# A hybrid attention and RG-LRU block: the T blocks of X made by four operations and begun sooner, the first chunks of X loaded once, three of seven low parts made by GpSimd in the second half

## The chip, the core and the metric

One core of one Trainium2 chip. The metric is device time in microseconds. Engines are named as in the profile: PE (TensorE matmuls), PEld (its weight loads), DVE (VectorE), ACT (ScalarE), POOL (GpSimd), SP (SyncE, which here only issues DMAs).

## The reference

The core of what is computed, for x of (1, 2048, 1024):

```python
proj = x @ w_in[l] + b_in[l]                    # 1024 -> 9216 columns: q, k, v, two SiLU gates, LRU input, merge gates
q, k, v, g_attn, u_lru, g_lru, gate_logits = jnp.split(proj, SPLIT_POINTS, axis=-1)
...                                             # rotary q and k, dilated banded attention for 3 groups of 8 heads
y_a = attn @ w_attn_proj[l]
u = causal_depthwise_conv(u_lru, conv_w[l], conv_b[l])
h = rg_lru(u, ...)                              # gates, then a scan over positions
y_b = (h * jax.nn.silu(g_lru)) @ w_lru_proj[l]
gates = jax.nn.sigmoid(gate_logits).reshape(B, S, N_BRANCHES, D)
merged = gates[:, :, 0] * y_a + gates[:, :, 1] * y_b
x = layer_norm(DEEPNORM_ALPHA * x + merged @ w_out[l] + b_out[l], ln_gain[l], ln_bias[l])
```

The change lies in the first line, the projection; everything behind it stays as it is.

## The kernel before, in words

The kernel runs in stages: the projection (to about 1555 us), attention, the two output projections with the gates, and the last product with the layer norm. Only the projection matters here.

**Products.** The 9216 columns are 72 strips of 128. Two strips make a pair, and the positions are taken in two halves of 1024, each of two chunks of 512; so the plan has 72 pairs, 0 to 35 for the first half and 36 to 71 for the second. Of a pair, weights (two strips by two halves of the inner dimension: A11, A12, A21, A22) and X (two halves of the inner dimension by two chunks: B11, B12, B21, B22) are 2 by 2 blocks. The first pair of each half is done plainly in eight products. All others take seven, by the scheme of Strassen and Winograd: `UNIT` and `BLK` give for product numbers 1 to 7 the weight block (A11, A12, S4, A22, S1, S2, S3) and the X block (B11, B21, B22, T4, T1, T2, T3). S1 to S4 and T1 to T4 are sums of blocks. The order of a pair's products is a tuple: `MID = (1, 6, 7, 5, 2, 4, 3)`, and `EDGE` for a half's last pair. In this document the first, second, ... seventh product of a pair is counted in that order.

**High and low parts.** For accuracy each block is split into a rounded high part (ACT copies it) and a low part (DVE or POOL subtracts). A product is twelve matmuls in `product` (L605): for each of four K tiles of 128, high by high, high by low, and the low part of the weights by high. So the low part of a weight block, tile `l`, is wanted by the third matmul of its product. Four `l` buffers hold two low parts each.

**The clock of the program.** One product is one tick. Per tick the code issues the product, then the events planned for it, then what chains (rotary products, gates, LRU) have come due, then the evacuation of PSUM. Each engine runs its own queue in this order, without a scheduler; events are put at ticks by hand (`at`). For a pair whose first product is at tick b, weights are loaded on SP ten to six ticks before (`load_w`); S1 and S3 are made by DMAs that accumulate into a loaded block, issued by POOL (`added`); `sums` makes S2 (DVE) and S4 (DVE in the first half, POOL in the second); `prep_w` makes high and low part of one unit per tick, four ticks ahead of its product in the first half, three in the second.

**Low parts of the second half.** In the first half `prep_w` makes the low parts (POOL the even ones, DVE the odd ones) and stores them to DRAM, `wl_scr`: two of 512 x 128 fp32 each (512 KB) after units 1, 3 and 5 and one (256 KB) after unit 6, counted from 0. In the second half `load_lo` (L290) reads them back, issued on SP for units 0, 2, 4 and 6; no low part of these pairs is computed.

**T blocks.** `comb` takes one K tile of the four raw blocks (tiles `xcB`) and makes T1, T2, T3 and the raw T4 with five sums on DVE, three copies on ACT, two low parts on POOL (T1, T3) and one on DVE (T2). `fourth` splits T4 later. At the start, the raw chunks for this are loaded a second time (`comb_loads`, 16 loads of 256 KB), four K tiles over ticks 0 to 3, and the four `comb` stand at ticks 3 to 6. At the change of halves, E0 is seven ticks before pair 36; loads stand at E0 + 6 to 9 and `comb` at E0 + 9 to 12.

Of the kernel before, what the change touches and what calls it, by code (L numbers as in the profile page):

```python
# [15 lines left out]
P = 128  # L16
# [4 lines left out]
CH = 512  # L21
# [10 lines left out]
def hybrid_block_kernel(ctx: ExitStack, tc: tile.TileContext, a: dict, out: bass.AP):  # L32
# [3 lines left out]
    def flat(t):  # L36
        return t.bitcast(F32)
# [13 lines left out]
    qk_scr = {(n, u): dram.tile([P, S], F32, name=f"{n}_scr{u}") for u in range(12) for n in ("qh", "ql", "k")}  # L51


    wl_scr = [dram.tile([P, 7, CH], F32, name=f"wl_scr{p}") for p in range(36)]
    u_scr = [dram.tile([P, CH], F32, name=f"u_scr{i}") for i in range(8)]


# [50 lines left out]
    def later(lag, fn):  # L108
        late.append((now["n"] + lag, fn))
# [23 lines left out]
    XSLOT = {"B11": "X2", "B21": "X3", "T2": "X4", "T3": "X5", "T1": "X1", "T4": "X0", "B12": "X0", "B22": "XA"}  # L133

    PLAIN = [(fi, k, c) for c in range(2) for fi in range(2) for k in range(2)]
    MID, EDGE = (1, 6, 7, 5, 2, 4, 3), (1, 2, 6, 7, 4, 5, 3)

    stA = ctx.enter_context(ExitStack())
    sl_p = stA.enter_context(tc.tile_pool(name="sl_p", bufs=1))
# [14 lines left out]
    def give(*ts):  # L154
        for t in ts:
            vacant.append(home.pop(id(t))[0])
# [69 lines left out]
        sp.dma_start(r, a["xT"][:, kx, c * CH:(c + 1) * CH])  # L226

    def drop_raw(b, kk):
        give(xr.pop((b, kk)))

    def tt(eng, out, in0, in1, op):
        eng.tensor_tensor(out=out, in0=in0, in1=in1, op=op)  # L232
# [30 lines left out]
    def prep_w(s, j):  # L263

        n = units_of(s)[j]
        r = raw.pop((s, n))
        h = take(f"h{n}_{s}")
        act.activation(h, r, AF.Copy)  # L268
        spend(ACT=.66)
        if (s, j // 2) not in LO:  # L270
            LO[s, j // 2] = take_lo(f"l{j}_{s}")
        l = LO[s, j // 2][1][:, j % 2]
        if plan[s][2] is None or not plan[s][0]:
            eng = pool if j % 2 == 0 else dve
            tt(eng, l, r, flat(h), ALU.subtract)
            if eng is pool:
                spend(POOL=1.55)
            else:
                spend(DVE=.93)
        give(r)  # L280
        U[s, n] = (h, l)
        if plan[s][2] and not plan[s][0] and (j % 2 or j == 6):
            jj = j - j % 2
            t = LO[s, j // 2][1][:, 0:j - jj + 1]
            later(2, lambda: sp.dma_start(wl_scr[plan[s][3]][:, jj:j + 1], flat(t)))

    def load_lo(s, j):
        t = LO[s, j // 2] = take_lo(f"l{j}_{s}")
        n = 1 if j == 6 else 2
        sp.dma_start(flat(t[1][:, 0:n]), wl_scr[plan[s][3]][:, j:j + n])  # L290
# [247 lines left out]
    plan = []  # L538
    for h in range(2):
        for p, (kind, f0, f1) in enumerate(seq):  # L540
            plan.append((h, ((f0, kind), (f1, kind)), None if p == 0 else EDGE if p == len(seq) - 1 else MID, p, kind))
# [113 lines left out]
    def at(t, fn):  # L655
        events.setdefault(t, []).append(fn)

    for s in range(1, NQ):
        t0 = base[s] - (3 if plan[s][0] else 4)
        if plan[s][2] is None:  # L660
            for d, n in ((4, "A21"), (4, "A11"), (3, "A22"), (3, "A12")):
                at(t0 - d, lambda s=s, n=n: load_w(s, n))
            for j in range(4):
                at(t0 + j, lambda s=s, j=j: prep_w(s, j))
            continue
        for d, n in ((6, "S1"), (6, "S3"), (4, "A11"), (3, "A22"), (3, "A12")):
            at(t0 - d, lambda s=s, n=n: load_w(s, n))
        at(t0 - 4, lambda s=s: added(s, "S1", "A22"))
        at(t0 - 4, lambda s=s: added(s, "S3", "A11"))
        at(t0 - 1, lambda s=s: sums(s))  # L670
        for j in range(7):
            if plan[s][0] and j % 2 == 0:
                at(t0 + j - 1, lambda s=s, j=j: load_lo(s, j))
            at(t0 + j, lambda s=s, j=j: prep_w(s, j))
    for s, pl in enumerate(plan):
# [23 lines left out]
    def comb(kk):  # L699
        r11, r12, r21, r22 = (xr["c" + b, kk] for b in ("B11", "B12", "B21", "B22"))  # L700
        if kk == 0:
            for n in ("T1", "T2", "T3"):
                new_block(n)
        tt(dve, r11, r11, r12, ALU.subtract)
        tt(dve, r12, r22, r12, ALU.subtract)
        hi_lo("T1", kk, r11, pool)
        tt(dve, r21, r11, r21, ALU.subtract)
        hi_lo("T3", kk, r12, pool)
        tt(dve, r11, r11, r22, ALU.add)
        hi_lo("T2", kk, r11, dve)  # L710
        tt(dve, r21, r21, r22, ALU.add)
        for b in ("B11", "B12", "B22"):
            drop_raw("c" + b, kk)
        spend(ACT=2.0, DVE=4.3, POOL=2.8)

    def fourth(kk):
        if kk == 0:
# [122 lines left out]
    for b in ("B12", "B22"):  # L840
        for kk in K4:
            load_raw(b, 1, kk)
    early = events
    events = {}
    prep_w(0, 0)
# [1 line left out]
        one_block("B11", 0, kk, some(kk))  # L847
    at(0, lambda: prep_w(0, 1))
    at(0, lambda: [one_block("B21", 0, kk, some(kk)) for kk in K4])
    at(0, lambda: comb_loads(0, 0))  # L850
    at(1, lambda: prep_w(0, 2))
    at(1, lambda: comb_loads(0, 1))
    at(1, lambda: prep_w(0, 3))
    at(2, lambda: [one_block("B12", 1, kk, some(kk)) for kk in K4])
    at(2, lambda: comb_loads(0, 2))
    at(3, lambda: [one_block("B22", 1, kk, some(kk)) for kk in K4])
    at(3, lambda: comb_loads(0, 3))
    for kk in K4:
        at(3 + kk, lambda kk=kk: comb(kk))
    at(7, lambda: [fourth(kk) for kk in K4])  # L860
# [519 lines left out]
```

## Time and profile before

| | us |
|---|---|
| median of 3 runs | 2367.07 |
| lowest, highest | 2362.84, 2371.19 |
| the profiled execution | 2367.64 |
| its span | 2365.8 |
| PE busy | 2243.7 (95%) |
| DVE, ACT, POOL busy | 1726.1 (73%), 1084.9 (46%), 1014.7 (43%) |
| DMA moved | 551.48 MB, 233 GB/s |

The profile is of one execution. A timeline row gives start and duration in us, engine, line, operation, what it writes and reads, and in brackets how long the engine stood idle before it and what ended that. A row of waits gives the total, the number and the longest. Matmul durations overlap: three of 0.39 us each start within 0.68 us.

### The profile page before, as it was taken

The numbers are of one execution on the slowest core, as the hardware profiler recorded it, in microseconds if no ns is written. First come the engines' busy times: TensorE is split into PE (matmuls) and PEld (weight loads), VectorE is DVE, ScalarE is ACT, GpSimd is POOL, SyncE is SP. The second block draws the span as 40 slices with busy tenths as digits, with TensorE's granted clock in tenths as the row PEclk, the third lists the DMA queues.
The fourth block names the chain that finished last, engine by engine and source line by source line (L and its number), as shares of the span: only waits on it lengthen the run. The fifth ranks groups of instructions, "written<-read, shape, count | busy, mean of one in ns | idle before, by whom it ended". The sixth has DMA issues, their size and how long they took to land.

```text
span 2365.8 us, 34610 instructions
## 1 busy us (share of the span) xinstructions
PE 2243.7 (95%) x11008; PEld 1878.5 (79%) x11008; DVE 1726.1 (73%) x3116; ACT 1084.9 (46%) x1977; POOL 1014.7 (43%) x760
## 2 busy tenths in 40 slices
PE   6999999999999799999999999989999999979998
PEld 4788888888788687787787877779999878758886
DVE  7888888899888676676667777546666558857677
ACT  4346445455465455465456665446666611121100
POOL 5554554456545433223232232368666326532220
PEclk8999999999999899999999999989999999999999
DMA  6888997988988987898897888897886579874431
GB/s 237 238 260 236 271 286 230 265 258 265 269 260 295 287 245 229 240 245 233 230 252 244 268 241 255 253 255 191 214 211 162 162 233 304 269 241 155 157 116 63
DMA packets 347174, 551.48 MB, mean 233 GB/s; under 512 B 99056, under 2 KB 140016, under 8 KB 342384
## 3 DMA queue, kind: packets, MB, share of 16 engines
q1 hardware_dynamic: 308160, 489.80, 66.2%
q0 software_dynamic: 20160, 36.71, 9.5%
q10 hardware_dynamic: 18672, 22.75, 3.1%
q8 instruction: 88, 1.44, 0.3%
q14 instruction: 94, 0.77, 0.1%
HBM read 343.81 MB, written 180.16 MB: 221 GB/s over the span
## 4 chain that ended last, share of the span: by engine, by line
PE 61%; DMA 13%; DVE 10%; issue 7%; POOL 4%; ACT 3%; SPq 2%; ACTq 0%; DVEq 0%; POOLq 0%
PE q L605 43%; DMA l<-wl_scr 4%; PE o L978 3%; PE s L939 2%; DMA A<-qh_scr 2%; PE pt L954 1%; PE yb L1167 1%; PE yb L1168 1%; PE yb L1166 1%; PE z L1260 1%; PE z L1258 1%; PE z L1259 1%; DVE xcB L232 1%; POOL C L789 1%; DMA wA<-in_w_in_dram 1%
## 5 line engine op out<-in xcount | busy, mean ns | idle before, releaser
L605 PE MATMUL q<-xT,hS 128*128 128x512 f32 x1680 | 523.3, 393 | 10.5 <-ACT hS L268 6.1
L605 PE MATMUL q<-xT,l 128*128 128x512 f32 x1120 | 438.9, 392 | 3.2 <-DVE l L232 3.2
L605 PE MATMUL q<-xB,hA 128*128 128x512 f32 x1248 | 398.7, 401 | 19.1 <-ACT hA L268 11.5
L605 PE MATMUL q<-xB,l 128*128 128x512 f32 x904 | 362.2, 401 | 36.8 <-DMA l<-wl_scr 28.2
L605 PEld LDWEIGHTS q<-xT,hS 128*128 128x128 f32 x1680 | 317.0, 189 | 78.7 <-ACT hS L268 7.1
L605 PEld LDWEIGHTS q<-xB,hA 128*128 128x128 f32 x1248 | 240.5, 194 | 70.6 <-ACT hA L268 12.3
L605 PEld LDWEIGHTS q<-xT,l 128*128 128x128 f32 x1120 | 211.7, 189 | 48.9 <-DVE l L232 4.3
L605 PEld LDWEIGHTS q<-xB,l 128*128 128x128 f32 x904 | 173.9, 192 | 81.4 <-DMA l<-wl_scr 35.1
L945 ACT ACTIVATE p<-p,osb 128x256 f32<-128x256 f32 (+1 forms) x384 | 156.5, 455 | 114.1 <-DVE osb L943 113.4
L232 POOL TENSOR_TENSOR sw<-sw,sin 128x512 f32<-128x512 f32 x96 | 159.8, 1681 | 98.6 <-DMA sw<-y 96.5
L943 DVE CUSTOM_DVE_ANT_0 p<-s,mask 128x256 f32<-128x256 f32 (+1 forms) x384 | 125.1, 364 | 100.4 <-PE s L939 59.6
L250 POOL DMA_DIRECT2D wS<-in_w_in_dram x140 | 123.8, 994 | 169.8 <-DMA wS<-in_w_in_dram 103.0
L268 ACT ACTIVATE hA<-wA 128x512 fp32r<-128x512 f32 x218 | 134.9, 623 | 95.3 <-DMA wA<-in_w_in_dram 51.1
L605 PE MATMUL q<-xB,hS 128*128 128x512 f32 x560 | 175.4, 394 | 2.1 <-DVE v L232 2.0
L605 PE MATMUL q<-xT,hA 128*128 128x512 f32 x560 | 174.1, 392 | 0.2 <-DVE u L232 0.2
L978 PE MATMUL o<-V,ptb 128*128 128x65 f32 x1200 | 165.0, 276 | 9.7 <-ACT ptb L959 7.8
L232 POOL TENSOR_TENSOR S<-S,wA 128x512 f32<-128x512 f32 x35 | 50.1, 1433 | 281.6 <-DVE S L232 116.3
L978 PEld LDWEIGHTS o<-V,ptb 128*128 128x128 f32 x1200 | 151.7, 194 | 21.4 <-ACT ptb L959 19.4
L232 DVE TENSOR_TENSOR y<-y,cos 128x512 f32<-128x512 f32 x96 | 121.3, 1267 | 48.6 <-DMA sw<-y 48.3
L232 POOL TENSOR_TENSOR l<-wA,hA 128x512 fp32r<-128x512 f32 x74 | 116.6, 1576 | 55.7 <-ACT hA L268 37.7
L1232 POOL TENSOR_TENSOR me<-gA,ybr 128x512 f32<-128x512 f32 x32 | 47.8, 1507 | 180.1 <-DVE gA L1231 177.6
L605 PEld LDWEIGHTS q<-xB,hS 128*128 128x128 f32 x560 | 104.3, 189 | 24.8 <-issue 2.9
(190 smaller groups left out, 4995.2 us busy)
## 6 DMA issues: line engine op xcount, KB each, us to landing
wA<-in_w_in_dram SPq DMA_DIRECT2D x218, 256.0 KB, 5.6
wl_scr<-l SPq DMA_DIRECT2D x105, 512.0 KB, 4.9
l<-wl_scr SPq DMA_DIRECT2D x105, 512.0 KB, 6.2
wS<-in_w_in_dram SPq DMA_DIRECT2D x140, 256.0 KB, 4.9
wS<-in_w_in_dram POOLq DMA_DIRECT2D x140, 256.0 KB, 7.0
sw<-y SPq DMA_DIRECT2D x384, 64.0 KB, 3.7
mg_scr<-y SPq DMA_DIRECT2D x59, 256.0 KB, 5.9
o_scr<-osb ACTq DMA_DIRECT2D x48, 264.0 KB, 5.9
```

Of the source, the lines that this page charges most:

```text
L232: eng.tensor_tensor(out=out, in0=in0, in1=in1, op=op)
L250: pool.dma_start(t, w_part(s, x), accum_op=ALU.add)
L268: act.activation(h, r, AF.Copy)
L605: pe.matmul(bank, w[:, ks], x[:, kk, xx], start=(first and i == 0), stop=(last and i == 11))
L789: pool.tensor_tensor(out=b2[hs, h, t], in0=flat(b2[hs, h, t]), in1=flat(B1[hs, h, t]), op=ALU.subtract)
L939: pe.matmul(s[:, h, (0 if g == 2 and n else lo):256], q, k, start=(i == 0), stop=(i == 1))
L943: dve.tensor_tensor_reduce(out=p[:, h, lo:256], in0=s[:, h, lo:256], in1=mask[:, lo:256], scale=1.0, scalar=3e38, op0=ALU.add, op1=ALU.min ...
L945: act.activation(p[:, h, lo:256], p[:, h, lo:256], AF.Exp, scale=-1.0, bias=mm)
L954: pe.transpose(pt[:, 2 * h + x, :], p[:, h, x * P:(x + 1) * P], ident)
L978: pe.matmul(o[:, n % 2, h * 65:h * 65 + 65], ptb[:, 2 * h + x, :], V[:, kb, vo + h * 65:vo + h * 65 + 65], start=(x == lo // P), stop=(x = ...
L1166: pe.matmul(yb, WL[f][:, 0, k], xx[:, 0], start=(k == 0), stop=False)
L1232: pool.tensor_tensor(out=ME[c][:, f], in0=ga, in1=yb, op=ALU.add)
```

## The change

- The pair after a plain one (pairs 1 and 37) takes the order `FIRST = (1, 2, 6, 7, 5, 4, 3)`: B21 before T2.
- `comb` makes the T blocks with four sums: T2 goes into B22's raw tile, and the raw T4 is T2 - B21. T1's low part goes to DVE and POOL in turn.
- At the start the raw chunks are kept and `comb` reads them; the second loads go. The blocks B12 and B22 are split one tick sooner, and `added` for pair 1 stands at tick 2 instead of 0. `comb` stays at ticks 3 to 6.
- At the change of halves loads for `comb` and `comb` stand two ticks sooner.
- In the second half units 0, 1 and 6 get their low part from POOL; only units 2 to 5 are stored and read back.

```diff
-    wl_scr = [dram.tile([P, 7, CH], F32, name=f"wl_scr{p}") for p in range(36)]
+    wl_scr = [dram.tile([P, 4, CH], F32, name=f"wl_scr{p}") for p in range(36)]
-    MID, EDGE = (1, 6, 7, 5, 2, 4, 3), (1, 2, 6, 7, 4, 5, 3)
+    MID, EDGE, FIRST = (1, 6, 7, 5, 2, 4, 3), (1, 2, 6, 7, 4, 5, 3), (1, 2, 6, 7, 5, 4, 3)
...
     def drop_raw(b, kk):
-        give(xr.pop((b, kk)))
+        t = xr.pop((b, kk))
+        if xr.get(("c" + b, kk)) is not t:
+            give(t)
...
         l = LO[s, j // 2][1][:, j % 2]
-        if plan[s][2] is None or not plan[s][0]:
-            eng = pool if j % 2 == 0 else dve
+        if plan[s][2] is None or not plan[s][0] or j in (0, 1, 6):
+            eng = pool if j % 2 == 0 or plan[s][0] and plan[s][2] else dve
             tt(eng, l, r, flat(h), ALU.subtract)
...
-        if plan[s][2] and not plan[s][0] and (j % 2 or j == 6):
-            jj = j - j % 2
-            t = LO[s, j // 2][1][:, 0:j - jj + 1]
-            later(2, lambda: sp.dma_start(wl_scr[plan[s][3]][:, jj:j + 1], flat(t)))
+        if plan[s][2] and not plan[s][0] and j in (3, 5):
+            t = LO[s, j // 2][1]
+            later(2, lambda: sp.dma_start(wl_scr[plan[s][3]][:, j - 3:j - 1], flat(t)))
...
-        n = 1 if j == 6 else 2
-        sp.dma_start(flat(t[1][:, 0:n]), wl_scr[plan[s][3]][:, j:j + n])
+        sp.dma_start(flat(t[1]), wl_scr[plan[s][3]][:, j - 2:j])
...
-        at(t0 - 4, lambda s=s: added(s, "S1", "A22"))
-        at(t0 - 4, lambda s=s: added(s, "S3", "A11"))
+        for n, x in (("S1", "A22"), ("S3", "A11")):
+            at(max(t0 - 4, 2), lambda s=s, n=n, x=x: added(s, n, x))
...
-            if plan[s][0] and j % 2 == 0:
+            if plan[s][0] and j in (2, 4):
                 at(t0 + j - 1, lambda s=s, j=j: load_lo(s, j))
...
         tt(dve, r11, r11, r12, ALU.subtract)
         tt(dve, r12, r22, r12, ALU.subtract)
-        hi_lo("T1", kk, r11, pool)
-        tt(dve, r21, r11, r21, ALU.subtract)
+        tt(dve, r22, r11, r22, ALU.add)
+        hi_lo("T2", kk, r22, dve)
+        tt(dve, r21, r22, r21, ALU.subtract)
         hi_lo("T3", kk, r12, pool)
-        tt(dve, r11, r11, r22, ALU.add)
-        hi_lo("T2", kk, r11, dve)
-        tt(dve, r21, r21, r22, ALU.add)
+        hi_lo("T1", kk, r11, some(kk))
...
-        at(E0 + 6 + kk, lambda kk=kk: comb_loads(2, kk))
-        at(E0 + 9 + kk, lambda kk=kk: comb(kk))
+        at(E0 + 4 + kk, lambda kk=kk: comb_loads(2, kk))
+        at(E0 + 7 + kk, lambda kk=kk: comb(kk))
...
+    for b in ("B11", "B21", "B12", "B22"):
+        for kk in K4:
+            xr["c" + b, kk] = xr[b, kk]
...
-    at(0, lambda: comb_loads(0, 0))
     at(1, lambda: prep_w(0, 2))
-    at(1, lambda: comb_loads(0, 1))
+    at(1, lambda: [one_block("B12", 1, kk, some(kk)) for kk in K4])
     at(1, lambda: prep_w(0, 3))
-    at(2, lambda: [one_block("B12", 1, kk, some(kk)) for kk in K4])
-    at(2, lambda: comb_loads(0, 2))
-    at(3, lambda: [one_block("B22", 1, kk, some(kk)) for kk in K4])
-    at(3, lambda: comb_loads(0, 3))
+    at(2, lambda: [one_block("B22", 1, kk, some(kk)) for kk in K4])
```

What this moves in the queues, at three places. In the rows `l2_0` is the low part of unit 2 of pair 0, `wS1_1` the block loaded for S1 of pair 1, `S4_37` the sum S4 of pair 37; a raw tile of X carries block, chunk and K tile.

POOL at the start, before: the low part for product 2 of pair 0 stands behind the two accumulating DMAs.

```order
L221 TENSOR_TENSOR xB21_287<-xB2101_232,xB21_287 128x512
L221 TENSOR_TENSOR xB21_287<-xB2103_236,xB21_287 128x512
L250 DMA wS1_1_304<-in_w_in_dram 128x512
L250 DMA wS3_1_306<-in_w_in_dram 128x512
L232 TENSOR_TENSOR l2_0_326<-wA21_0_238,hA21_0_324 128x512
L221 TENSOR_TENSOR xB12_358<-xB1211_244,xB12_358 128x512
L221 TENSOR_TENSOR xB12_358<-xB1213_248,xB12_358 128x512
```

The same place on POOL after the change:

```order
L221 TENSOR_TENSOR xB21_287<-xB2101_232,xB21_287 128x512
L221 TENSOR_TENSOR xB21_287<-xB2103_236,xB21_287 128x512
L234 TENSOR_TENSOR l2_0_316<-wA21_0_238,hA21_0_314 128x512
L221 TENSOR_TENSOR xB12_318<-xB1211_244,xB12_318 128x512
L221 TENSOR_TENSOR xB12_318<-xB1213_248,xB12_318 128x512
L221 TENSOR_TENSOR xB22_349<-xB2211_252,xB22_349 128x512
L221 TENSOR_TENSOR xB22_349<-xB2213_256,xB22_349 128x512
L252 DMA wS1_1_296<-in_w_in_dram 128x512
L252 DMA wS3_1_298<-in_w_in_dram 128x512
```

The low part now comes right behind B21's; the two DMAs stand behind B22's.

POOL at the change of halves, before: pair 37 has only its sum S4 here, in the middle of the T blocks.

```order
L221 TENSOR_TENSOR xT3_7437<-xcB1231_7384,xT3_7437 128x512
L232 TENSOR_TENSOR S4_37_7500<-S2_37_7498,wA12_37_7433 128x512
L221 TENSOR_TENSOR xT1_7435<-xcB1122_7406,xT1_7435 128x512
L221 TENSOR_TENSOR xT3_7437<-xcB1232_7408,xT3_7437 128x512
L221 TENSOR_TENSOR xT1_7435<-xcB1123_7449,xT1_7435 128x512
L221 TENSOR_TENSOR xT3_7437<-xcB1233_7451,xT3_7437 128x512
```

The same place on POOL after the change:

```order
L221 TENSOR_TENSOR xT3_7294<-xcB1233_7307,xT3_7294 128x512
L221 TENSOR_TENSOR xT1_7292<-xcB1123_7305,xT1_7292 128x512
L234 TENSOR_TENSOR S4_37_7408<-S2_37_7406,wA12_37_7356 128x512
L234 TENSOR_TENSOR l0_37_7426<-wA11_37_7325,hA11_37_7424 128x512
L234 TENSOR_TENSOR l0_37_7426<-wA12_37_7356,hA12_37_7445 128x512
```

S4 now stands behind the last T low part, and the low parts for the first two products of pair 37 stand behind S4.

POOL in the second half, before, from S4 of pair 44 to S4 of pair 45:

```order
L232 TENSOR_TENSOR S4_44_8842<-S2_44_8840,wA12_44_8794 128x512
L250 DMA wS1_45_8891<-in_w_in_dram 128x512
L250 DMA wS3_45_8893<-in_w_in_dram 128x512
L232 TENSOR_TENSOR S4_45_9046<-S2_45_9044,wA12_45_8991 128x512
L232 TENSOR_TENSOR y49_2_8686<-y49_2_8686,h1_2_9015 128x512
```

The same place on POOL after the change:

```order
L234 TENSOR_TENSOR l0_44_8759<-wA11_44_8658,hA11_44_8757 128x512
L234 TENSOR_TENSOR l0_44_8759<-S2_44_8737,hS2_44_8784 128x512
L252 DMA wS1_45_8789<-in_w_in_dram 128x512
L252 DMA wS3_45_8791<-in_w_in_dram 128x512
L234 TENSOR_TENSOR l6_44_8940<-S4_44_8739,hS4_44_8938 128x512
L234 TENSOR_TENSOR S4_45_8944<-S2_45_8942,wA12_45_8889 128x512
L234 TENSOR_TENSOR l0_45_8970<-wA11_45_8852,hA11_45_8968 128x512
```

Two low parts stand between S4 and the next pair's accumulating DMAs, and a third between these and the next S4.

More of the change, by code (lines that the diff above doesn't have):

```diff
@@ L540, in hybrid_block_kernel @@
         for p, (kind, f0, f1) in enumerate(seq):
-            plan.append((h, ((f0, kind), (f1, kind)), None if p == 0 else EDGE if p == len(seq) - 1 else MID, p, kind))
+            plan.append((h, ((f0, kind), (f1, kind)), None if p == 0 else EDGE if p == len(seq) - 1 else FIRST if p == 1 else MID, p, kind))
     NQ = len(plan)
@@ L705, in comb @@
         tt(dve, r12, r22, r12, ALU.subtract)
-        hi_lo("T1", kk, r11, pool)
-        tt(dve, r21, r11, r21, ALU.subtract)
+        tt(dve, r22, r11, r22, ALU.add)
+        hi_lo("T2", kk, r22, dve)
+        tt(dve, r21, r22, r21, ALU.subtract)
         hi_lo("T3", kk, r12, pool)
-        tt(dve, r11, r11, r22, ALU.add)
-        hi_lo("T2", kk, r11, dve)
-        tt(dve, r21, r21, r22, ALU.add)
+        hi_lo("T1", kk, r11, some(kk))
         for b in ("B11", "B12", "B22"):
             drop_raw("c" + b, kk)
-        spend(ACT=2.0, DVE=4.3, POOL=2.8)
+        spend(ACT=2.0, DVE=4.0, POOL=2.1)
     def fourth(kk):
```

## The prediction

> **What bounds the kernel now.** I read the windows view first, then the waits of TensorE, then the timeline at the places where TensorE stands still.
>
> ```profile
> span 2365.8 us, 34610 instructions
> 0.00:50.00 50.00, 30.96 (x108) 23.81 (x108) 36.09 (x40) 19.96 (x33) 26.60 (x28) 0.90 0.72 248
> 50.00:100.00 50.00, 42.24 (x160) 32.86 (x161) 37.77 (x61) 19.46 (x35) 25.99 (x21) 0.90 0.74 215
> 150.00:750.00 600.00, 596.80 (x2664) 491.54 (x2663) 534.05 (x633) 302.24 (x503) 316.91 (x233) 1.00 0.87 259
> 750.00:800.00 50.00, 37.97 (x157) 30.51 (x155) 38.42 (x42) 23.99 (x41) 32.10 (x22) 0.86 0.93 310
> 805.00:1551.00 746.00, 717.24 (x3132) 586.57 (x3132) 503.30 (x670) 408.19 (x667) 226.08 (x180) 0.98 0.86 247
> ```
>
> A row gives the stretch, its length, busy time with instruction counts of PE, PEld, DVE, ACT and POOL, then granted clock, DMA share and GB/s. Through 150 to 750 PE is busy for 596.80 of 600 us at full clock: the projection is bound by matmuls there, and only its gaps can be won. They are in three places that the change touches: the first 100 us (268 matmuls, where 150 to 750 does 222 per 50 us), the change of halves (157 in 50 us), and the second half (28.8 us idle, and 2% of the clock, 15 us: some 43 us).
>
> ```profile
> PE q L605 <- DMA l<-wl_scr: 28.2, 14, 3.5
> 914.40 0.50 PE L605 MATMUL q<-xB,l 128*128 128x512 f32 x1 [1.59 <-DMA l<-wl_scr]
> 925.32 0.80 PE L605 MATMUL q<-xB,l 128*128 128x512 f32 x1 [2.45 <-DMA l<-wl_scr]
> 1173.33 0.50 PE L605 MATMUL q<-xB,l 128*128 128x512 f32 x1 [3.54 <-DMA l<-wl_scr]
> 1234.72 0.50 PE L605 MATMUL q<-xB,l 128*128 128x512 f32 x1 [0.95 <-DMA l<-wl_scr]
> 1402.01 0.50 PE L605 MATMUL q<-xB,l 128*128 128x512 f32 x1 [2.36 <-DMA l<-wl_scr]
> 1503.97 0.50 PE L605 MATMUL q<-xB,l 128*128 128x512 f32 x1 [2.53 <-DMA l<-wl_scr]
> ```
>
> In the second half PE waits for one thing, the low parts read back from DRAM: 14 waits, 28.2 us (us in total, times, longest). Counting twelve matmuls to a product, four fall on a pair's first product (first 925.32, last 1173.33; some 11 us), two on its seventh (1234.72 and 1402.01; 3.3 us), eight on its fifth (first 914.40, last 1503.97; the other 14 us).
>
> **The start.** The page's times are of one execution of 2367.64 us, 0.6 us above the median of 2367.07; sums are made against the first.
>
> ```profile
> 10.76 3.27 POOL L221 TENSOR_TENSOR xB<-xB,xB 128x512 fp32r<-128x512 f32 x2 [0.72 <-ACT xB L220]
> 21.82 1.90 POOL L250 DMA_DIRECT2D wS<-in_w_in_dram  x2 [7.79 <-DMA wS<-in_w_in_dram]
> 23.11 1.91 POOL L232 TENSOR_TENSOR l<-wA,hA 128x512 fp32r<-128x512 f32 x1
> 5.80 0.80 PE L605 MATMUL q<-xB,hA 128*128 128x512 f32 x1 [5.80 <-ACT xB L220]
> 16.12 0.61 PE L605 MATMUL q<-xB,hA 128*128 128x512 f32 x2
> 25.07 0.79 PE L605 MATMUL q<-xB,l 128*128 128x512 f32 x1 [8.34 <-POOL l L232]
> 25.00:30.00 5.00, 4.93 (x12) 3.87 (x13) 5.00 (x1) 0.00 (x0) 5.00 (x6) 0.50 1.10 291
> 36.64 0.39 PE L605 MATMUL q<-xB,l 128*128 128x512 f32 x1
> 37.32 0.39 PE L605 MATMUL q<-xB,l 128*128 128x512 f32 x1
> 77.27 0.70 PE L605 MATMUL q<-xB,hS 128*128 128x512 f32 x2 [0.78 <-DVE v L232]
> ```
>
> Three matmuls take 0.68 us (36.64 to 37.32), a product 2.72. The row at 77.27 opens the last product of pair 1, with 14 products before it: 38 us of work. From the first matmul at 5.80 that is 71.5 us, 33 of them lost.
>
> Product 2 waits because its low part stands on POOL behind two accumulating DMAs, and these wait 7.79 us for loads queued behind chunks of X that are read twice. After the change the low part stands ahead of both: POOL is free at 14.03, 1.3 us later it is done, before PE wants it. That takes away 8.5 us, and the 12 matmuls at clock 0.50 behind it (5 us for 2.7): **11 us**. The eight plain products then end at 16.4 + 6 x 2.72 = 32.7.
>
> ```profile
> 20.67 0.69 DVE L221 TENSOR_TENSOR xB<-xB,xB 128x512 fp32r<-128x512 f32 x1 [0.34 <-ACT xB L220]
> 46.40 2.93 POOL L221 TENSOR_TENSOR xT<-xcB,xT 128x512 fp32r<-128x512 f32 x2 [1.90 <-ACT xT L220]
> 43.26 3.72 DVE L232 TENSOR_TENSOR xcB<-xcB,xcB 128x512 f32<-128x512 f32 x4
> 48.14 1.73 DVE L232 TENSOR_TENSOR xcB<-xcB,xcB 128x512 f32<-128x512 f32 x1 [1.16 <-POOL xT L221]
> 50.57 0.69 DVE L221 TENSOR_TENSOR xT<-xcB,xT 128x512 fp32r<-128x512 f32 x1 [0.70 <-ACT xT L220]
> 51.18 0.68 DVE L232 TENSOR_TENSOR xcB<-xcB,xcB 128x512 f32<-128x512 f32 x1
> ```
>
> Then the T blocks set the pace. One K tile takes DVE 7.9 us (43.26 to 51.18): sums at 0.93, a wait for POOL, which still reads the tile that the next sum overwrites, that sum at 1.73, a wait for ScalarE's copy, the low part. In the new order T2 goes into a tile that nobody else reads: three sums (2.8), the wait (0.7), the low part (0.6), the fourth sum (0.9), and every other time T1's low part (0.3 on average): **5.3 us**. They can begin behind the last low part of B22 (20.67, or 1 us sooner). Four take 21 us, and the sums of pair 1 stand behind the first and will wait some 2.5 us for the accumulation that POOL now issues later: done at about 44, where it was 59. The second half of that gain is not kept: T2's own weights have their low part on POOL behind T3's and T1's last tile, 3 x 1.3 us, so T2's product, now third in pair 1, gets it at about 48. Four more products (10.9), and 1 us for the next low part on POOL: the last product of pair 1 starts at about 60, **17 us sooner**. It gives 10 if the accumulations land 3 us later still and the 7 us of small softplus instructions on DVE hold an evacuation; 23 if POOL's queue does not bind. On SP 16 loads (4 MB) go, so pair 1's weight loads stand right behind B22's.
>
> **The change of halves.**
>
> ```profile
> 772.33 0.69 DVE L232 TENSOR_TENSOR xcB<-xcB,xcB 128x512 f32<-128x512 f32 x1 [2.64 <-DMA xcB<-in_xT_dram]
> 786.88 1.65 POOL L232 TENSOR_TENSOR S<-S,wA 128x512 f32<-128x512 f32 x1 [3.22 <-DVE S L232]
> 793.65 1.22 PE L605 MATMUL q<-xB,hA 128*128 128x512 f32 x2 [10.99 <-ACT hA L268]
> 801.07 0.73 PE L605 MATMUL q<-xT,hS 128*128 128x512 f32 x2 [2.11 <-ACT hS L268]
> ```
>
> The sums start when their chunk has landed (772.33). Asked for two products sooner, it lands only some 2 us sooner, since the DMA engines are at 0.93 here already. (Two groups of X now stand ahead of pair 37's weights on SP; at 310 GB/s their 2 MB are 7 us, and S2 is not wanted for 20.) Four tiles of 5.3 us end at about 791.6. What comes late next is new: pair 37's first low part stands on POOL behind S4, S4 behind S2 on DVE, and S2 behind the last T sum. 0.6 + 1.65 + 1.3 us: the third matmul runs at about 796, where it was 794.7. The second wait (2.11, and a colder clock) goes, T2 being one product later. Net **2 us**, from -3 (POOL's queue later still) to 8 (sums at the 0.69 of an undisturbed one).
>
> **The second half.**
>
> ```profile
> L232 POOL TENSOR_TENSOR l<-wA,hA 128x512 fp32r<-128x512 f32 x74 | 116.6, 1576 | 55.7 <-ACT hA L268 37.7
> l<-wl_scr SPq DMA_DIRECT2D x105, 512.0 KB, 6.2
> 1275.59 1.29 POOL L232 TENSOR_TENSOR S<-S,wA 128x512 f32<-128x512 f32 x1 [6.96 <-DMA wA<-in_w_in_dram]
> 1279.59 0.39 PE L605 MATMUL q<-xB,l 128*128 128x512 f32 x1
> 936.51 1.29 POOL L232 TENSOR_TENSOR S<-S,wA 128x512 f32<-128x512 f32 x1 [6.98 <-DVE S L232]
> 906.67 0.53 SPq L290 DMA_DIRECT2D l<-wl_scr  x1
> SPq L290 <- PE q L605: 78.2, 41, 5.5
> ```
>
> Removed in each of 35 pairs: the loads for products 1, 2 and 7 (768 KB of 1792), and as much written in the first half. Added: three low parts on POOL, 105 x 1.58 = 166 us, so POOL goes from 226 to 392 us of 746, or 0.53, its share in 150 to 750. The waits of first and seventh product go with their loads: 14.3 us. The new cover is POOL's queue. In the tight pair above, S4 ends at 1276.9, so the low part behind it is there at 1278.3, and PE reads it at 1279.59; in the pair of 936.51 it would be there at 939.2, for a product at 947.7. Behind a late one stand the next accumulations and the rotary products on POOL, and behind these DVE's sums; I take 4 us of new waits. The eight waits of the fifth product stay in kind: its load left SP at 906.67 and was used at 914.40, 7.7 us, against 6.2 in the median. SP has two fewer loads per pair to issue, which also stood still for PE to free a buffer (78.2 us in 41 waits), and there is less on the wire: I take half, 7 us, between 0 and 14. The clock's 15 us follow the waits: 8. Sum 14 + 7 + 8 - 4 = **25 us**, from 8 (fifth product unchanged, new waits on POOL) to 40 (nearly all of 43). The first half has 3.2 us idle; fewer stores give **1**, from 0 to 3.
>
> A rule that speaks against this: the Trainium skill's page "SBUF — State Buffer", section "SBUF: two separate sides", has VectorE and GpSimd share a port pair as an exclusive lock, so that a GpSimd operation blocks a VectorE operation with two SBUF inputs for its whole length. By it the 105 operations could take 105 x 1.3 = 134 us from DVE. The trace agrees in kind (DVE's sum takes 0.69 at 772.33, and 1.73 at 48.14 beside POOL's two from 46.40). It does not change the sum: DVE would go from 503 to 637 of 746 us, 0.85, and at 534 of 600 in 150 to 750 PE loses nothing.
>
> **The sum.** 17 + 2 + 25 + 1 = 45 us: 2367.6 - 45 = 2322.6, and 2322 on the scale of the median.
>
> **Rivals.**
> - SP stays as late as before (0.25): the fifth product's waits remain, and the seventh's low part, on POOL behind rotary products that wait for the same SP queue, gives back a third of the rest. The second half gives 8, all in all 28: 2339. For it: the waits come in clusters where SP is late.
> - Every low part on time (0.14): second half 40, start 20, together 63: 2304.
> - Slower (0.05): POOL's queue becomes the bound. If S4 and the low parts behind it come on average 1.5 us after PE wants them, 35 pairs cost 52 us, the second half's 25 are gone, and 20 remain: 2400. It decides from 0.6 us per pair. Against it: the tight pair has 1.3 us to spare, the other 8.
> - The port lock in the path (0.02): DVE's evacuations late by as much as POOL holds the port, 134 us less 20: 2480. Against it: 150 to 750.
> - The T blocks are not begun sooner in effect (0.04): weights and POOL hold pair 1 as before, only the 11 us of product 2 remain, the change of halves gives 0: 2331.
>
> **How the numbers follow.** The forecast has 0.50. Its terms at their ends give 15 to 74 us, so 2293 to 2352; the range 2290 to 2352 takes in the first, second and last rival, and leaves out the slower ones and the tails of the others, under 2 in 10. A measurement of this kernel tells 0.3%, 7 us, from no change. Faster by more: 0.90 (forecast, first, second and last rival, less their tails); within it 0.04; slower 0.06.
>
> **What would show it.** The third product without a wait for POOL at the start; the last product of pair 1 at 55 to 66 us; PE's wait at the change of halves for POOL's low part, no more for ScalarE's copy; in the second half no waits for loads on first and seventh products, fewer on fifth ones, and POOL near 390 us. It is wrong if TensorE waits for POOL's low parts by more than some 10 us after 805, or if pair 1 ends where it did.

## The result, and the profile after

The changed kernel took 2366.11 us (median of 12, from 2362.33 to 2375.34), the kernel before 2367.49 in the same runs (2360.47 to 2372.97). The ratio is 1.001, 95% interval 0.9993 to 1.0026: no change, where 2322 us had been forecast.

The first view is the windows view of the changed kernel, in the stretches shown of before, with the span:

```profile
span 2365.2 us, 34453 instructions
0.00:50.00 50.00, 33.78 (x122) 25.39 (x122) 39.63 (x48) 25.31 (x44) 28.46 (x29) 0.97 0.58 185
50.00:100.00 50.00, 46.22 (x183) 37.52 (x184) 38.37 (x58) 15.96 (x30) 29.22 (x24) 0.90 0.76 210
150.00:750.00 600.00, 599.73 (x2684) 496.11 (x2683) 543.31 (x636) 308.97 (x512) 325.41 (x237) 1.00 0.80 227
750.00:800.00 50.00, 37.47 (x152) 29.95 (x151) 34.36 (x36) 21.70 (x40) 29.27 (x23) 0.86 0.88 280
805.00:1551.00 746.00, 705.48 (x3072) 575.74 (x3070) 551.32 (x661) 400.80 (x654) 373.52 (x276) 0.97 0.77 205
```

Up to 100 us there are 305 matmuls now, 37 more; up to 800 the kernel is well ahead. In the last row PE has lost: 705.48 us busy of 746, where it had 717.24. DVE has gone from 503.30 to 551.32 us, with the same work to do: POOL's 105 low parts are the only thing that was added here. The waits of TensorE from 805 to 1551 (total, times, longest), and then its rows in the timeline that answer to those of before; L937 is attention's first matmul:

```profile
PE q L605 <- DMA l<-wl_scr: 34.5, 10, 6.7
```

```profile
67.32 0.70 PE L605 MATMUL q<-xB,hS 128*128 128x512 f32 x2 [2.06 <-DVE u L234]
779.36 1.22 PE L605 MATMUL q<-xB,hA 128*128 128x512 f32 x2 [9.83 <-ACT hA L270]
783.28 0.79 PE L605 MATMUL q<-xB,l 128*128 128x512 f32 x1 [2.70 <-POOL l L234]
903.65 0.80 PE L605 MATMUL q<-xB,l 128*128 128x512 f32 x1 [5.66 <-DMA l<-wl_scr]
1551.44 0.30 PE L937 MATMUL s<-B,A 128*128 128x128 f32 x1 [3.22 <-DMA A<-qh_scr]
1556.52 0.58 PE L937 MATMUL s<-B,A 128*128 128x256 f32 x1 [3.57 <-DVE osb L941]
```

In the kernel before, the row that answers to that of 1551.44 (in both kernels two small matmuls come ahead of it) was:

```profile
1555.11 0.30 PE L939 MATMUL s<-B,A 128*128 128x128 f32 x1 [3.23 <-DMA A<-qh_scr]
```

Where the lead comes and goes can be read from these rows and those before. The last product of pair 1 starts 10.0 us sooner (67.32, was 77.27). The wait that opens pair 37 begins 13.1 us sooner (779.36 - 9.83, was 793.65 - 10.99), and pair 37 starts 14.3 us sooner. Attention starts only 3.7 us sooner (1551.44 against 1555.11): the second half gave 10.6 us back. A wait for DVE in attention's first steps (1556.52) and what follows take the other 3.1. Of the ten waits for low parts read back, 34.5 us where it was 28.2 in 14, nine now stand on fifth products (33.8 us) and a short one on a third (0.75 us, at 1420.29); none is left on first and seventh ones.

So two parts work against each other, and the question is why the second half lost 11 us where three of seven reads were taken out of it.

### The profile page after: what moved, and what is told of

Its sections match the earlier page's. It is cut to its first block, busy times and chain, and to the rows that moved or that the text cites. A ratio compares the mean times of both kernels' runs of the same rounds, so it can differ in the third digit from the quotient of the medians.

```text
span 2365.2 us, 34453 instructions
## 1 busy us (share of the span) xinstructions
PE 2242.4 (95%) x11008; PEld 1879.4 (79%) x11008; DVE 1780.9 (75%) x3112; ACT 1082.7 (46%) x1977; POOL 1169.7 (49%) x861
## 4 chain that ended last, share of the span: by engine, by line
PE 27%; DMA 7%; issue 5%; DVE 5%; ACT 3%; POOL 2%; SPq 1%; ACTq 0%; DVEq 0%; POOLq 0%
PE q L605 8%; PE o L976 4%; PE s L937 3%; PE yb L1165 2%; PE yb L1166 2%; PE yb L1164 2%; PE pt L952 2%; PE z L1258 1%; PE z L1256 1%; PE z L1257 1%; DMA l<-wl_scr 1%; DMA A<-qh_scr 1%; POOL me L1230 1%; DMA ybr<-yb_scr 1%; ACT p L943 1%
## 5 line engine op out<-in xcount | busy, mean ns | idle before, releaser
L605 PE MATMUL q<-xB,l 128*128 128x512 f32 x904 | 362.5, 401 | 40.7 <-DMA l<-wl_scr 33.8
L234 POOL TENSOR_TENSOR l<-S,hS 128x512 fp32r<-128x512 f32 x105 | 160.2, 1526 | 324.6 <-ACT hS L270 206.0
L234 POOL TENSOR_TENSOR l<-wA,hA 128x512 fp32r<-128x512 f32 x110 | 173.1, 1575 | 61.1 <-ACT hA L270 47.8
L605 PEld LDWEIGHTS q<-xT,hA 128*128 128x128 f32 x560 | 106.3, 191 | 24.3 <-issue 1.9
```

Of the source, the lines that this page charges most:

```text
L605: pe.matmul(bank, w[:, ks], x[:, kk, xx], start=(first and i == 0), stop=(last and i == 11))
```

## The experiments

**The theories.** A1: the fifth product's low parts are asked for late, because their load stands on SP behind rotary swaps (`sw<-y`), which wait for DVE's outputs `y`. A2: DVE is late because POOL's 105 operations slow it. Rivals: C (the low parts cost nothing, the lead is lost in attention), D (the load is bound by the wire), E (the chains' budgets changed the order), F (POOL's own queue), G (a price only from some number of low parts on).

Four kernels ran at a time, beside the kernel before on one chip; its median was 2355.4, 2356.2 and 2364.8 us there. So ratios are compared, each to the kernel before in its own group (with the 95% interval), and times only within a group. "Second half" is the time from the start of pair 37's first product to the start of the projection's last matmul, read off each trace: 757.7 us before, 768.3 after. The window from 805 to 1551 is the same for all; in the quicker kernels the projection ends at 1510 to 1534, and the rest of the window is attention.

### One part at a time

The first kernel is the change with W's low parts as before, the second the kernel before with that part alone:

```diff
-        if plan[s][2] is None or not plan[s][0] or j in (0, 1, 6):
-            eng = pool if j % 2 == 0 or plan[s][0] and plan[s][2] else dve
+        if plan[s][2] is None or not plan[s][0]:
+            eng = pool if j % 2 == 0 else dve
...
-            if plan[s][0] and j in (2, 4):
+            if plan[s][0] and j % 2 == 0:
                 at(t0 + j - 1, lambda s=s, j=j: load_lo(s, j))
```

> The change without its part on W's low parts: all seven are made in the first half, stored and read back as before; T blocks and first chunks as in the change. Theory A (the second half gives back what start and change of halves gain): the 13 us that the projection is ahead at its 261st product stay, 2354 us, and the second half waits for low parts by 28 us in 14 waits as before. Rival C (the low parts cost nothing and the 13 us are lost at the end anyway, where the attention's first steps wait for stored rows): 2366.

Measured: ratio 0.9951 (0.9933 to 0.997), second half 746.1 us, 25.2 us in 12 waits.

> The kernel before with the part on the low parts alone: three of seven made by PoolE in the second half. Theory A: start and change of halves as before, the second half loses some 10 us, 2377 us, its waits for low parts read back being on fifth products alone, some 35 us. Rival C: 2367. What I had forecast for this part, 25 us of gain: 2342.

Measured: ratio 1.0086 (1.0066 to 1.0105), second half 768.5 us. The blocks gain 0.5%, the low parts lose 0.9%, and together they give the 0.1% of the change within the intervals. Rival C falls. The 25 us that I had forecast for the low parts were a loss of 20; Theory A, too, had said only 10.

### The load issued sooner

```diff
-                at(t0 + j - 1, lambda s=s, j=j: load_lo(s, j))
+                at(t0 + 1, lambda s=s, j=j: load_lo(s, j))
```

> The change, with the load of the fifth product's low parts issued two products sooner, together with the third product's, ahead of the rotary swaps of two outputs on SyncE's queue. Theory A1 (the fifth product waits because its load is issued late, behind swaps that wait for VectorE's sums): TensorE's waits for low parts go from 34.5 us to under 10, 2340 to 2345 us. Rival D (the transfer itself takes as long as the wire lets it; issuing sooner only queues it): waits stay above 25, 2360 or more.

Measured: ratio 1.0011 (0.9998 to 1.0024), as slow as the change, second half 762.2. Both theories fall. The waits of this kernel from 805 to 1551:

```profile
PE q L605 <- DVE u L234: 10.5, 6, 2.6
PE q L605 <- DVE v L234: 4.9, 4, 1.6
PE q L605 <- POOL l L234: 3.5, 5, 1.4
PE q L605 <- DMA l<-wl_scr: 1.2, 1, 1.2
```

And its timeline at the place of 903.65 above, of PE and then of DVE:

```profile
903.29 1.04 PE L605 MATMUL q<-xT,hA 128*128 128x512 f32 x2 [2.64 <-DVE u L234]
```

```profile
896.94 2.01 DVE L234 TENSOR_TENSOR y<-y,cos 128x512 f32<-128x512 f32 x1 [4.45 <-DMA sw<-y]
901.85 0.69 DVE L234 TENSOR_TENSOR y<-y,cos 128x512 f32<-128x512 f32 x1 [1.70 <-DMA sw<-y]
902.46 0.68 DVE L234 TENSOR_TENSOR u<-e,q 128x512 f32<-128x512 f32 x1
```

The load did come in time: 1.2 us are left of 34.5, so D is wrong. But PE now waits for DVE to empty its PSUM bank (`u<-e,q`), one product later. That sum stands on DVE behind two rotary products, and these wait 4.45 and 1.70 us for swaps that left late: SP had stood 14.1 us for the first of the four outputs, sent its swap at 883.94, and issued without a stop of 1 us from there. A1 saw one branch of this. The late thing is the output; the load and the sum behind the swap both hang on it.

### PoolE's operations taken away, and what it is about them

In the first of these the 105 low parts are left out (the third matmul takes the high part); in the second, three memsets stand in the place of each. The order is that of the change in both. The edits, one behind the other:

```diff
-            tt(eng, l, r, flat(h), ALU.subtract)
+            if not (plan[s][0] and plan[s][2]):
+                tt(eng, l, r, flat(h), ALU.subtract)
...
-        U[s, n] = (h, l)
+        U[s, n] = (h, h if plan[s][0] and plan[s][2] and j in (0, 1, 6) else l)
```

```diff
-            tt(eng, l, r, flat(h), ALU.subtract)
+            if plan[s][0] and plan[s][2]:
+                for _ in range(3):
+                    pool.memset(flat(l), 0.0)
+            else:
+                tt(eng, l, r, flat(h), ALU.subtract)
```

> The change with the 105 low parts that PoolE makes in the second half left out, its order of instructions kept otherwise: the third matmul of a first, second and seventh product takes the high part of W in place of the low one, so the output is not the reference's. Theory A2 (PoolE's 105 operations slow VectorE, whose late sums hold the swaps and so the load): VectorE's busy time from 805 to 1551 falls from 551 to some 505 us, waits for low parts to 15 or less, some 2345 us. Rival E (the new order of the chains, from the budgets that the three low parts take, puts the swaps in the load's way): waits stay near 34 us in 10, some 2363.

Measured: ratio 0.9919 (0.9905 to 0.9934), second half 738.2; 20.8 us in 10 waits, where A2 had said 15 or less; DVE busy 511.19 us from 805 to 1551. The order was that of the change, so E falls.

> The change with each of the 105 low parts that PoolE makes in the second half replaced by three memsets of its tile: they fill PoolE's queue at the same places for about the same time, but read nothing from SBUF (the third matmul then multiplies by zeros, so the output is not the reference's). Theory A2 (PoolE's reading of two SBUF tiles slows VectorE's operations on two SBUF tiles): VectorE's sums take 0.69 us again, its busy time from 805 to 1551 falls from 551 to some 511 us, waits for low parts read back to about 21 us, and the time is some 0.8% under the kernel before, as with the operations left out. Rival F (what costs is PoolE's queue: sums, accumulations and rotary products stand behind the low parts): VectorE's operations may be quicker, but the time stays within 0.2% of the kernel before.

Measured: ratio 0.9924 (0.9895 to 0.9953), second half 740.9. The waits and the window from 805 to 1551 of the version with memsets:

```profile
PE q L609 <- DMA l<-wl_scr: 18.2, 9, 4.4
```

```profile
805.00:1551.00 746.00, 721.28 (x3271) 595.73 (x3270) 507.51 (x734) 417.30 (x693) 393.22 (x489) 0.98 0.80 215
```

Three groups on DVE from 805 to 1530 (busy us, mean ns), with memsets and then in the change:

```profile
L456 DVE SCALAR_TENSOR_TENSOR v<-ub,lrn,v 128x512 f32<-128x512 f32 x57 | 42.8, 752 | 15.7 <-ACT v L454 14.2
L234 DVE TENSOR_TENSOR sq<-sq,ti 128x512 f32<-128x512 f32 x20 | 14.8, 740 | 0.7
L555 DVE SCALAR_TENSOR_TENSOR y<-q,bn,v 128x512 f32<-128x512 f32 x36 | 26.8, 745 | 19.0 <-PE q L609 18.8
```

```profile
L452 DVE SCALAR_TENSOR_TENSOR v<-ub,lrn,v 128x512 f32<-128x512 f32 x57 | 51.5, 903 | 14.4 <-ACT v L450 13.0
L234 DVE TENSOR_TENSOR sq<-sq,ti 128x512 f32<-128x512 f32 x20 | 18.7, 935 | 0.7
L551 DVE SCALAR_TENSOR_TENSOR y<-q,bn,v 128x512 f32<-128x512 f32 x36 | 26.7, 742 | 16.2 <-PE q L605 16.2
```

POOL is as busy as in the change (393.22 us against 373.52), at the same places in its queue, and the loss is gone: F falls, A2 stands. What costs is that POOL reads SBUF. DVE's operations on two SBUF tiles take 0.94 and 0.90 us beside the subtractions, 0.74 and 0.75 beside the memsets; those that read one operand from PSUM (`y<-q,bn,v`) take 0.74 in both. The price is 0.88% between change and memsets (1.0012, as measured again below, less 0.9924), 21 us, by the two intervals some 8 more or less.

Two other readings of this run don't hold by the traces. A memset doesn't wait for ACT's copy, as a subtraction does, so POOL's queue is held less; but DVE does not wait longer for POOL in the change (`rp<-y,sw` for POOL's `sw`: 11.5 us in 5 waits, 18.0 in 7 with memsets). And matmuls with zeros might have raised the clock; but the kernel whose third matmul takes the high part is as fast (0.9919), and the clock granted over the run was 0.982 in the profiles of both.

The same burst in the timelines shows how it gets from there to PE. Pair 41 gives its outputs `y` to DVE in four successive products, between operations of an LRU chain; in the change (the first and the third output):

```profile
881.50 1.59 DVE L501 SCALAR_TENSOR_TENSOR tr<-tr,e 128x512 f32<-128x512 f32 x1
883.02 0.74 DVE L551 SCALAR_TENSOR_TENSOR y<-q,bn,v 128x512 f32<-128x512 f32 x1
884.94 1.11 DVE L505 SCALAR_TENSOR_TENSOR sq<-sq,e 128x512 f32<-128x512 f32 x1
886.08 1.67 DVE L234 TENSOR_TENSOR sq<-sq,ti 128x512 f32<-128x512 f32 x1
887.67 0.74 DVE L551 SCALAR_TENSOR_TENSOR y<-q,bn,v 128x512 f32<-128x512 f32 x1
```

POOL at the same time, and SP behind it:

```profile
880.82 1.73 POOL L234 TENSOR_TENSOR S<-S,wA 128x512 f32<-128x512 f32 x1
882.51 1.74 POOL L234 TENSOR_TENSOR l<-wA,hA 128x512 fp32r<-128x512 f32 x1
884.21 1.29 POOL L234 TENSOR_TENSOR y<-y,h 128x512 f32<-128x512 f32 x1
885.46 1.74 POOL L234 TENSOR_TENSOR l<-S,hS 128x512 fp32r<-128x512 f32 x1
```

```profile
883.82 2.48 SPq L310 DMA_DIRECT2D sw<-y  x4
893.61 3.04 SPq L310 DMA_DIRECT2D sw<-y  x4
896.75 0.81 SPq L290 DMA_DIRECT2D l<-wl_scr  x1
```

With memsets the same operations on DVE, the first swap and the load on SP, and the matmul on PE that waits for it:

```profile
877.29 0.69 DVE L505 SCALAR_TENSOR_TENSOR tr<-tr,e 128x512 f32<-128x512 f32 x1
877.90 0.74 DVE L555 SCALAR_TENSOR_TENSOR y<-q,bn,v 128x512 f32<-128x512 f32 x1
879.82 0.68 DVE L509 SCALAR_TENSOR_TENSOR sq<-sq,e 128x512 f32<-128x512 f32 x1
880.53 0.69 DVE L234 TENSOR_TENSOR sq<-sq,ti 128x512 f32<-128x512 f32 x1
881.82 0.75 DVE L555 SCALAR_TENSOR_TENSOR y<-q,bn,v 128x512 f32<-128x512 f32 x1 [0.60 <-PE q L609]
```

```profile
878.71 2.48 SPq L314 DMA_DIRECT2D sw<-y  x4
890.94 0.63 SPq L294 DMA_DIRECT2D l<-wl_scr  x1
```

```profile
898.25 0.50 PE L609 MATMUL q<-xB,l 128*128 128x512 f32 x1 [1.52 <-DMA l<-wl_scr]
```

Three LRU operations take 4.37 us beside POOL (1.59, 1.11, 1.67) and 2.06 with memsets. Only the third stands beside a low part alone; the first overlaps the sum `S` and then a low part, the second `y<-y,h` and then a low part, and both kernels have this sum and this product. With memsets DVE waits 0.60 us for the third output's product; in the change it comes to it with a backlog, without idle time. That backlog is older than these rows: three LRU steps `v<-ub,lrn,v` from 860.74 took 4.26 us beside two low parts on POOL, and 2.32 us from 858.24 beside six memsets.

What sets the load is the first output. In the change DVE takes it at 883.02, 5.7 us after PE went on to the next product (877.37); with memsets at 877.90, 1.8 us after (876.11). SP stands for it with the swap at the head of its queue, 14.2 us in the change, and sends that swap at 883.82 and 878.71. From there SP issues one transfer behind another, without a stop of 1 us, until the fifth product's load leaves, 12.9 and 12.2 us later: at 896.75, 1.2 us before PE wants it (903.65 - 5.66 = 897.99); with memsets at 890.94, 5.8 us before (898.25 - 1.52). This is one of the ten waits; the others were not followed in this way.

### How many low parts

```diff
-        if plan[s][2] is None or not plan[s][0] or j in (0, 1, 6):
+        if plan[s][2] is None or not plan[s][0] or j == 6:
...
```

> The change with one low part of seven made by PoolE in the second half (that of the seventh product) and six read back. If the price is paid per operation (theory A2, 105 of them cost about 30 us and their loads were worth 8), a third of it: 0.3% under the kernel before, 5 us more than the version with blocks only. Rival G (a price only from some load of VectorE on): 0.5% under, like the version with blocks only.

Measured: ratio 0.9956 (0.9934 to 0.9977), second half 747.5, DVE busy 530.06 us from 805 to 1551.

The same with `j in (0, 1)`, beside the change once more:

> The change with two low parts of seven made by PoolE in the second half, those of the first and second products, and five read back. These two fall on the three products in which the pair ahead hands VectorE its four outputs and PoolE their rotary products; the seventh's falls elsewhere. Theory A3 (what a low part on PoolE costs depends on where it falls: those beside the outputs cost nearly everything): 0.1% under to 0.2% over the kernel before, like the whole change. Rival G (it depends on how many there are, cheap up to some load): about 0.3% under, half way between the version with the seventh alone and the whole change.

> The changed kernel unaltered, on the chip of the three runs beside it, so that its trace can be set against theirs. All theories: within 0.3% of the kernel before, waits for low parts read back of some 34 us on fifth products.

Measured: 0.9951 (0.9933 to 0.9968) with first two, second half 753.8 and DVE 540.86; 1.0012 (0.9996 to 1.0027) for the change, 767.9 and 548.43. A3 falls: the two beside the outputs don't carry the price. With none, one, two, three low parts per pair on POOL the ratio is 0.9951, 0.9956, 0.9951, 1.0012. To within the 0.2% of the intervals, one or two cost no more than the loads that they replace are worth; the third costs 0.6%, 14 us, and in the traces of one group the second half takes 753.8 us with two and 767.9 with three. A price per operation would have put two near 0.999, which their interval shuts out (one alone does not: 0.997 lies in its interval). That is rival G in kind, though G had said 0.3% under for two. DVE's busy time doesn't jump at the third, with 514.20, 530.06, 540.86 and 548.43 us; what jumps is how much of it reaches PE. Why it does so isn't settled, nor whether the number decides or the company of the seventh with the other two, for no other two were tried.

### What does beat both

The reads of before are kept, and the loads for first, fifth and seventh products issued one, two and one products sooner; with the blocks, and on the kernel before alone:

```diff
-                at(t0 + j - 1, lambda s=s, j=j: load_lo(s, j))
+                at(t0 + (-2, 1, 1, 4)[j // 2], lambda s=s, j=j: load_lo(s, j))
```

> Blocks only (all low parts read back), with the loads of first, fifth and seventh products' low parts issued one, two and one products sooner. Theory A1 for a VectorE that isn't slowed: of 25 us of waits for low parts in 12 waits under 8 remain, and the time goes from 0.5% under the kernel before to some 1.1% under. Rival H (as in the change with its load two products sooner, VectorE's sums stand right behind, and TensorE waits for them instead): at most 5 us gained, 0.7% under.

Measured: ratio 0.9887 (0.9843 to 0.9932), second half 728.6:

```profile
PE q L607 <- DMA l<-wl_scr: 4.6, 6, 1.5
```

```profile
805.00:1551.00 746.00, 723.85 (x3299) 594.94 (x3298) 509.65 (x743) 420.06 (x700) 249.54 (x195) 0.99 0.89 254
```

With DVE at 509.65 us the waits fall from 25.2 to 4.6 us and the time by 0.6%, 15 us, where beside POOL's low parts taking them away gave nothing. Rival H's 0.7% under lies just inside the interval, but the waits for DVE that it rests on are 2.3 us in all. So the load's place on SP did cost, and did so in the kernel before already:

> The kernel before with the loads of first, fifth and seventh products' low parts issued one, two and one products sooner, and nothing of the change. If what this gives doesn't hang on the T blocks: waits for low parts from 28 us to under 8, 0.6% under the kernel before. Rival (without the 13 us that the blocks bring sooner, SyncE stands so far behind that sooner means nothing): 0.2% under or less.

Measured: ratio 0.991 (0.9878 to 0.9942), 7.4 us of such waits left. The rival falls; the first theory's 0.6% lies at the edge of the interval, and the measured gain is rather more.

And the version with the seventh's low part on POOL, its loads sooner:

```diff
             if plan[s][0] and j in (0, 2, 4):
-                at(t0 + j - 1, lambda s=s, j=j: load_lo(s, j))
+                at(t0 + (-2, 1, 1)[j // 2], lambda s=s, j=j: load_lo(s, j))
```

> The seventh's low part by PoolE, six read back with their loads issued sooner, T blocks as in the change. Theory A3 (the seventh's low part falls where VectorE has time): as fast as the same with all seven read back, 1.1% under the kernel before. Rival A2 with a price per operation: 0.8 to 0.9% under.

Measured: ratio 0.9885 (0.9855 to 0.9915), second half 734.4: as fast as with all seven read back, though the 0.991 of a price per operation lies just inside the interval.

The last adds two edits to the blocks with sooner loads (pair 37's loads for these two products, its sums and the accumulation of S1 move along, by three to five products):

```diff
...
-            at(t0 + j, lambda s=s, j=j: prep_w(s, j))
+            at(t0 + j - (3 if s == 37 and j < 2 else 0), lambda s=s, j=j: prep_w(s, j))
...
-    at(10, scales)
+    at(18, scales)
```

> As the version before, and two edits for the start and the change of halves: softplus of the parameters eight products later, and the weights of pair 37's first two products made ready three products sooner, ahead of the third K tile's T blocks. If each takes away what the trace shows (2.1 us of waiting for VectorE at 67.3; two products, 5.4 us, done inside the 13.5 us of waiting at the change of halves): 7 us more than without them, some 1.4% under the kernel before. If the T blocks end later by as much, only the 2 us.

Measured: ratio 0.9902 (0.9863 to 0.994), nothing gained. Its trace shows both waits again, elsewhere:

```profile
87.07 0.70 PE L607 MATMUL q<-xB,hA 128*128 128x512 f32 x2 [1.48 <-DVE u L234]
771.87 1.22 PE L607 MATMUL q<-xB,hA 128*128 128x512 f32 x2 [2.31 <-ACT hA L270]
783.35 1.22 PE L607 MATMUL q<-xB,hA 128*128 128x512 f32 x2 [7.03 <-ACT y L386]
```

Pair 37 starts at 771.87, but its second product waits 7.03 us for ACT to empty a bank, behind copies of the T blocks; the two waits are 9.34 us where the version without these edits waits 11.10 once. Softplus, moved, delays DVE's sum at 87. PE waits for DVE once more at 102.12 (1.20 us), but DVE has stood idle twice in between, so that this comes from softplus isn't shown.

## Why the prediction was wrong

- **The step that failed** is the last sentence on the Trainium skill's rule: "It does not change the sum: DVE would go from 503 to 637 of 746 us, 0.85, and at 534 of 600 in 150 to 750 PE loses nothing." The price on DVE's time was even smaller than that (551, not 637), yet it cost 21 us. The share of a stage was taken for slack at every place in it. At the burst of four outputs that was followed DVE had a backlog of 5.7 us where it had 1.8 with memsets, and what it had lost went to the outputs, to the swaps and to the load. In the first half DVE is busier, 543.31 of 600 us, and PE loses nothing; but no low part is read back there behind swaps (that this makes the difference is argued, not tried). In the same passage 105 x 1.3 is 136.5 and not 134, which changes nothing.
- **The term that failed with it** is "half of it, 7" for the fifth product. I gave SP the relief of fewer loads and forgot that the load's turn is set by the swaps ahead of it. Its waits went from 14 to 33.8 us. Even with memsets 18.2 us of waits for low parts were left, all on fifth products, so fewer loads gave these no relief that shows. Nor did the 8 us for the clock come: 0.97 was granted from 805 to 1551 (0.98 when the change was measured again), where it had been 0.98. The second half was +25 in the forecast; the runs give -20 for the low parts alone (1.0086), and some 8 of gain for fewer loads without POOL's reading (0.9951 less 0.9919; 5 by the medians).
- **What was right in it:** first and seventh products wait for no load, and after 805 PE waits for none of POOL's low parts. POOL was busy for 373.52 us, forecast 392. So neither of the two signs of being wrong that I had named came: both looked at POOL and at the start, and the loss went through DVE and SP.
- **The rivals.** The port lock in the path (0.02) was the right mechanism with a price six times too large: 134 us of blocking taken as 134 of delay. "SP stays as late" named the right queue and gave it no reason to be later than before.
- **The start:** +17 in the forecast, 10 measured. The third product's wait is gone as said. But one K tile of T blocks took more than the 5.3 us of the forecast: T2's low parts begin at 25.29, 32.51, 39.65 and 46.48, 7.1 us apart. I had counted the sums at 0.93 us, and four of them took 5.83 us beside three low parts on POOL, the slowing that the second half shows too (here read, not tested); pair 1's own sums and low part stand in between as well. So the low part of T2's weights came at 51.7 instead of 48, and the last product waited for DVE behind softplus, which ends on DVE at 65.25:

```profile
33.12 5.83 DVE L234 TENSOR_TENSOR xB<-xB,xB 128x512 f32<-128x512 f32 x4
33.07 2.94 POOL L221 TENSOR_TENSOR xT<-xB,xT 128x512 fp32r<-128x512 f32 x2 [5.92 <-ACT xT L220]
47.05 2.96 POOL L221 TENSOR_TENSOR xT<-xB,xT 128x512 fp32r<-128x512 f32 x2 [5.55 <-ACT xT L220]
49.96 1.72 POOL L234 TENSOR_TENSOR l<-S,hS 128x512 fp32r<-128x512 f32 x1
56.12 1.97 DVE L83 TENSOR_SCALAR spt<-lr 128x8 f32<-128x8 f32 x1
```

  Of the seven us that are missing 3.7 are in the third and fourth rows, where POOL can only begin T3's and T1's last low parts at 47.05, and 2.1 in the wait at 67.32; the rest lies behind the wait for the low part, where the granted clock was 0.51 from 51 to 58. These are read from the trace; that moving softplus gains nothing in the end, the run with it moved shows.
- **First half and change of halves:** 1 and 2 in the forecast, 3.1 and 1.2 by the rows. At the change of halves the third matmul of pair 37 runs 13.8 us after PE came to a stand (783.28, from 779.36 - 9.83); my 796 was 13.3 us after the same point of before (793.65 - 10.99). So the chain to POOL's low part behind S4 was about right. What I had left out is ACT's copy for the same product, which stands on ACT behind the last tile's T copies: 9.83 us of the wait end with it and only 2.70 with POOL.
- **Attention** lost 3.1 us, for which I had no term; what does that was not tried. A wait of 2.9 us for the same `osb` stands in the kernel with memsets too, so it does not hang on what POOL's low parts read.

The sum of the rows is 10.0 + 3.1 + 1.2 - 10.6 - 3.1 = 0.6 us, what the two spans differ by (2365.8 and 2365.2); attention's term is what was left over to make it so.

## What to carry to other kernels

An engine that is 70% busy over a stage can have no time left just where others wait for its results: ask for its backlog at that place, in the timeline, before work is put on a neighbour that slows it. When a wait names a load, look at what stands ahead of its issue; and before you move it, at who else hangs on the same late thing, since taking one wait away may only show the next. The cheap move was to issue the load sooner, not to do without it.

## What the runs showed of the hardware

A POOL subtraction of two SBUF tiles slows DVE's operations on two SBUF tiles (`sq<-sq,ti` 0.94 us on average instead of 0.74, single ones 1.67 instead of 0.69), and leaves those with a PSUM operand alone (0.74 on average in both, and 0.74 at 883.02 beside a subtraction). A POOL memset, which reads nothing, doesn't slow them: DVE's busy time in the stage was 507.51 us beside the memsets, 551.32 beside the subtractions. The Trainium skill's page "SBUF — State Buffer", section "SBUF: two separate sides", says this of the shared port pair: a VectorE operation with two SBUF inputs is locked out only by a GpSimd operation that reads SBUF. These traces agree, the memset included; the operations with a PSUM operand have one SBUF input.

That one and two such operations per pair cost no more than the loads that they replace are worth, and the third 14 us, I had not expected either.
